# In-place weight sums in the MLP and convolution, and a one-step normalisation after the convolution

## The chip, the core and the metric

The kernel runs on one core of a Trainium2 chip. The metric is the device time of one execution in microseconds. Before the change it is 2091.16 us (median of three runs, 2089.38 to 2091.38). The engines of the core are named as the profile names them: PE is TensorE (matrix products and transposes), DVE is VectorE, ACT is ScalarE, POOL is GpSimd, and SP is SyncE, which here only issues transfers.

## The reference

The model is a two-layer decoder trunk over 1024 tokens of width 1024, in float32. Layer 0 mixes tokens with a causal convolution module, layer 1 with sliding-window attention. Both are followed by a layer norm, a squared-ReLU MLP of width 4096, a second norm and a gated extra embedding. The parts that the change touches:

```python
h = x @ w_in + b_in
a, gate = jnp.split(h, 2, axis=-1)
h = a * jax.nn.sigmoid(gate)
h = depthwise_causal_conv(h, w_dw) + b_dw            # width 31
h = jax.nn.silu(layer_norm(h, ln_g, ln_b))           # the convolution's norm
y = h @ w_out + b_out
...
mlp = jnp.square(jax.nn.relu(x @ w_up)) @ w_down
```

with `layer_norm(x) = (x - mean) * rsqrt(var + 1e-5) * g + b`.

## The kernel before

**Products.** Each float32 operand is split into a rounded high part and a rest (`wh` and `wl` for weights, `xh` and `xl` for activations), and each product is made of three passes: high by high, high by low and low by high. So every weight tile passes through ACT (the cast to `wh`) and DVE (the subtraction `raw - wh`, which gives `wl`) before PE can use it. In the input product of the convolution and in the MLP's up product two blocks of weights are handled as a pair by a Strassen-like scheme with seven products instead of eight. That scheme needs sums of the pair's raw tiles.

**A pair of weights.** `pair_units` (line 1457) gives four units of work, `u0` to `u3`; a unit is one `wh` and one `wl` tile of 128 x 1024. The pair's tiles `raw[0]` and `raw[1]` are of 128 x 1024 too, and L and R are their left and right halves of 512 columns. `u0` splits `raw[0]` as it is, `u1` forms the first two sums, `u2` the third and fourth, `u3` splits the right half of `raw[1]`. Before the change all four sums go to tiles of 128 x 512 of the pool `g`, which has four slots; the pool `raw` has two. The inner function `slot` (line 1463) casts and subtracts each source by itself, so `u1` and `u2` cost two casts and two subtractions of 512 columns each. In the MLP five early pairs of blocks (`EARLY`, 0 to 8) make their `u0` product ahead of the rest; their `u1` loads both raw tiles anew (`again`). A unit's tiles come from rings of five slots.

**The order of products in the MLP.** For a pair, PE multiplies `u1`'s left half with the token form `T[2]` (tiles named X), `u2`'s left half with `T[3]` (E), `u1`'s right half with `T[1]` (A), `u2`'s right half with a plain quarter (`xh`, `xl`) and `u3` with `T[4]` (B): five groups of twelve matmuls, and two more groups for `u0` where the pair isn't early.

**The convolution's norm.** `conv_ln` (line 1264) runs once per pair of token tiles (four pairs, `t0` = 0, 2, 4, 6). A tile consists of two halves of 512 channels, `q` = 0 (tiles named X) and `q` = 1 (tiles named A). `stats` (line 741) takes the mean and variance with two BN_STATS and one BN_AGGR on DVE, adds epsilon and raises to -0.5 on POOL, and then makes the second scalar, -mean * rstd, with one SCALAR_TENSOR_TENSOR of 128 x 1 on DVE. Each half is then scaled in place as `z * rstd + (-mean * rstd)`, `q` = 0 on DVE and `q` = 1 on POOL. PE transposes the scaled halves, ACT applies Silu with the norm's gain and bias, and `xh` and `xl` come from DVE and ACT. Around that place PE fills its time with the product of the extra embedding (`wh`, `wl` by `wh`, `wl`) until the first blocks of the mixer's output product (`wh` by `xh`) can start.

**What sets the order.** Nothing is written out by hand. The program records all operations with their dependences, tile allocations among them, and a list scheduler (`schedule`, with the costs in `cost`) simulates the engines and gives each one a fixed order. Priority is the place in the program, moved by `later`, `after` and `slack`. A tile of a ring is allocated when the simulated schedule frees its slot. So an operation that is removed or shortened, or a tile that is held longer, can move what comes behind it on every engine. All recorded instructions carry one line in the profile, L496; they are told apart by tile names.

Of the kernel before, what the change touches and what calls it, by code (L numbers as in the profile page):

```python
# [13 lines left out]
ALU = mybir.AluOpType  # L14
# [6 lines left out]
HT = 512  # L21
# [507 lines left out]
class Emit:  # L529
# [208 lines left out]
            nc.tensor.matmul(ps, lh, rl, start=False, stop=False, **kw)  # L738
            nc.tensor.matmul(ps, ll, rh, start=False, stop=stop and i == n - 1, **kw)

    def stats(self, halves):

        nc = self.nc
        st = self.small(12).rearrange("p (a b) -> p a b", a=2)
        for i, s in enumerate(halves):
            nc.vector.bn_stats(st[:, i, :], s)
        mv = self.small(2)
        nc.vector.bn_aggr(mv, st)
        rs = self.small(2)
        nc.gpsimd.tensor_scalar(  # L750
            out=rs[:, 0:1], in0=mv[:, 1:2], scalar1=1.0, scalar2=EPS, op0=ALU.mult, op1=ALU.add
        )
        nc.gpsimd.tensor_tensor(out=rs[:, 0:1], in0=rs[:, 0:1], in1=self.mhalf, op=ALU.pow)
        nc.vector.scalar_tensor_tensor(
            out=rs[:, 1:2], in0=mv[:, 0:1], scalar=-1.0, in1=rs[:, 0:1], op0=ALU.mult, op1=ALU.mult
        )
        return rs
# [178 lines left out]
    def conv(self):  # L936

        nc, d, ws = self.nc, self.d, self.ws
# [325 lines left out]
        def conv_ln(t0):  # L1264

            zs = []
            for t in (t0, t0 + 1):
                z = [Z[t // 4, t % 4, q] for q in range(2)]
                rs = self.stats(z)
                for q in range(2):  # L1270
                    (nc.gpsimd if q else nc.vector).tensor_scalar(out=z[q], in0=z[q], scalar1=rs[:, 0:1], scalar2=rs[:, 1:2], op0=ALU.mult, op1=ALU.add)
                zs.append(z)
            for f in range(0, KB, 2):
                blk = [slice((f + j) % 4 * P, ((f + j) % 4 + 1) * P) for j in range(2)]
# [169 lines left out]
    def pair_units(self, aps, again=False):  # L1444

        nc = self.nc
# [3 lines left out]
        def slot(srcs, parts):  # L1450
            wh = nc.tile("wh", (P, 1024), F32R)
            wl = nc.tile("wl", (P, 1024), F32R)
            for s, c in zip(srcs, parts):
                nc.scalar.copy(wh[:, c], s)
                nc.vector.tensor_tensor(out=wl[:, c], in0=s, in1=wh[:, c].bitcast(F32), op=ALU.subtract)
            return wh, wl
# [19 lines left out]
            return slot((S[2], S[1]), (L, R))  # L1476

        def u2():
            S[3], S[4] = self.sb("g"), self.sb("g")
            nc.vector.tensor_tensor(out=S[3], in0=raw[0][:, L], in1=raw[1][:, L], op=ALU.subtract)  # L1480
            nc.vector.tensor_tensor(out=S[4], in0=raw[0][:, R], in1=S[2], op=ALU.subtract)
            return slot((S[3], S[4]), (L, R))

        def u3():
            return slot((raw[1][:, R],), (L,))
# [897 lines left out]
```

## Time and profile before

| what | value |
|---|---|
| three runs | 2091.38, 2091.16, 2089.38 us |
| the profiled execution: time / span | 2088.0 / 2086.3 us |
| busy PE, DVE, ACT, POOL | 2077.3, 1688.4, 1228.1, 279.1 us |
| matmuls and transposes on PE | 9784 |
| convolution up to its norm | 0 to about 256 us |
| the norm and the start of the mixer's output product | about 256 to 285 us |
| up product of the first MLP | about 370 to 690 us |
| up product of the second MLP | about 1395 to 1735 us |

The span runs from the first to the last instruction. The windows view gives, for each stretch, the busy time of each engine with its count of instructions in brackets, then the granted PE clock, the share of the DMA engines and the rate. The timeline view gives start, duration, engine, operation, output and inputs, form and count; what stands in square brackets is the idle time of the engine ahead of the row and what ended it. Matmuls overlap, so a row's duration is longer than the distance from one start to the next.

### The profile page before, as it was taken

How to read it: one execution, taken by the hardware profiler on the slowest of the kernel's cores; microseconds unless marked ns; L12 is line 12 of the kernel's file. 1: busy time of each engine (PE TensorE's matmuls, PEld its weight loads, DVE VectorE, ACT ScalarE, POOL GpSimd, SP SyncE). 2: the span in 40 equal slices, each digit the busy share in tenths (PEclk: the TensorE clock that was granted, in tenths of full speed). 3: DMA queues.
4: the chain of work that ended last, by engine and by line, in shares of the span. 5: the costliest groups of instructions: out<-in, count | busy, mean ns of one | idle time of the engine just before them, and what ended most of it. 6: DMA issues, size and time to landing. Idle time of an engine off the chain costs nothing.

```text
span 2086.3 us, 29471 instructions
## 1 busy us (share of the span) xinstructions
PE 2077.3 (100%) x9784; PEld 1730.8 (83%) x9784; DVE 1688.4 (81%) x2628; ACT 1228.1 (59%) x2268; POOL 279.1 (13%) x512
## 2 busy tenths in 40 slices
PE   9999999999999999999999999999999999999999
PEld 7888888888888888888888888888888888888877
DVE  8999796978876789986983677879888778888688
ACT  6777656856655644454752678866665663333374
POOL 0524121000000000001220356500000000000041
PEclk9999999999999999999999999999999999999999
DMA  6669855988986879876468685598788886575636
GB/s 227 189 205 300 284 192 183 341 289 284 305 308 192 309 269 316 274 261 244 166 219 296 230 291 195 190 337 301 274 295 299 287 298 202 185 245 171 237 112 206
DMA packets 249864, 521.96 MB, mean 250 GB/s; under 512 B 25456, under 2 KB 64112, under 8 KB 249712
## 3 DMA queue, kind: packets, MB, share of 16 engines
q1 hardware_dynamic: 246544, 517.99, 73.3%
q10 hardware_dynamic: 3168, 2.10, 0.3%
q8 instruction: 77, 1.26, 0.2%
q14 instruction: 75, 0.61, 0.1%
HBM read 348.81 MB, written 168.56 MB: 248 GB/s over the span
## 4 chain that ended last, share of the span: by engine, by line
PE 94%; ACT 2%; DVE 2%; DMA 1%; POOL 1%; issue 0%; SPq 0%; DVEq 0%; ACTq 0%
PE ps L496 71%; PE tr L496 23%; ACT z L496 1%; POOL sm L496 1%; ACT t L496 0%; DVE z L496 0%; DMA z<-in_w_dw_dram 0%; DMA A<-in_w_up_dram 0%; DMA mid<-A 0%; DVE B L496 0%; ACT xh L496 0%; DVE E L496 0%; POOL A L496 0%; DMA X<-in_xT_dram 0%; DVE t L496 0%
## 5 line engine op out<-in xcount | busy, mean ns | idle before, releaser
L496 PE MATMUL ps<-xh 128*128 128x512 f32 x618 | 240.4, 389 | 0.0
L496 PE MATMUL ps<-xl,xh 128*128 128x512 f32 x618 | 240.4, 389 | 0.0
L496 PE MATMUL ps<-xh,xl 128*128 128x512 f32 x618 | 240.4, 389 | 0.0
L496 POOL TENSOR_SCALAR sm<-sm 128x1 f32<-128x1 f32 x72 | 26.3, 368 | 1395.2 <-DVE E L496 1208.8
L496 PE MATMUL ps<-xh,wh 128*128 128x512 f32 x520 | 203.3, 393 | 0.8 <-ACT xh L496 0.5
L496 PE MATMUL ps<-xh,wl 128*128 128x512 f32 x520 | 203.4, 392 | 0.0
L496 PE MATMUL ps<-xl,wh 128*128 128x512 f32 x520 | 203.3, 391 | 0.0
L496 ACT CAST wh<-raw 128x1024 fp32r<-128x1024 f32 (+2 forms) x134 | 119.8, 894 | 84.0 <-PE ps L496 46.2
L496 PE MATMUL ps<-wh,xh 128*128 128x512 f32 (+1 forms) x368 | 144.7, 394 | 1.4 <-DVE t L496 0.9
L496 PE MATMUL ps<-wl,xh 128*128 128x512 f32 (+1 forms) x368 | 144.6, 393 | 0.0
L496 PE MATMUL ps<-wh,xl 128*128 128x512 f32 (+1 forms) x368 | 144.4, 392 | 0.0
L496 DVE TENSOR_TENSOR wl<-raw,wh 128x1024 fp32r<-128x1024 f32 (+2 forms) x100 | 98.7, 989 | 52.9 <-ACT wh L496 52.4
L496 ACT CAST wh<-g 128x512 fp32r<-128x512 f32 x136 | 81.1, 619 | 95.2 <-PE ps L496 41.0
L496 PEld LDWEIGHTS ps<-xl,xh 128*128 128x128 f32 x618 | 116.0, 188 | 24.2
L496 PEld LDWEIGHTS ps<-xh,xl 128*128 128x128 f32 x618 | 116.0, 188 | 24.0
L496 PEld LDWEIGHTS ps<-xh 128*128 128x128 f32 x618 | 116.0, 188 | 24.0
L496 ACT CAST xh<-wh 128x1024 fp32r<-128x1024 f32 x76 | 79.8, 1050 | 94.0 <-PE ps L496 56.0
L496 PEld LDWEIGHTS ps<-xh,wh 128*128 128x128 f32 x520 | 97.9, 188 | 21.2 <-ACT xh L496 0.9
L496 PEld LDWEIGHTS ps<-xl,wh 128*128 128x128 f32 x520 | 97.8, 188 | 20.4 <-DVE xl L496 0.8
L496 PEld LDWEIGHTS ps<-xh,wl 128*128 128x128 f32 x520 | 97.7, 188 | 19.8
L496 DVE TENSOR_TENSOR xl<-wh,xh 128x1024 fp32r<-128x1024 f32 x76 | 92.7, 1220 | 25.9 <-ACT xh L496 25.7
L496 ACT ACTIVATE t<-t 128x512 f32<-128x512 f32 x144 | 90.9, 632 | 35.1 <-DVE t L496 33.4
(408 smaller groups left out, 5641.1 us busy)
## 6 DMA issues: line engine op xcount, KB each, us to landing
wh<-hid SPq DMA_DIRECT2D x78, 512.0 KB, 4.7
raw<-in_w_up_dram SPq DMA_DIRECT2D x68, 512.0 KB, 4.4
wl<-in_w_down_dram SPq DMA_DIRECT2D x58, 512.0 KB, 5.3
hid<-zz SPq DMA_DIRECT2D x96, 256.0 KB, 4.8
hid<-t SPq DMA_DIRECT2D x64, 256.0 KB, 4.8
z<-in_w_dw_dram SPq DMA_DIRECT2D x56, 288.0 KB, 4.2
raw<-hid SPq DMA_DIRECT2D x30, 512.0 KB, 4.9
A<-mid SPq DMA_DIRECT2D x48, 256.0 KB, 4.7
```

What stands on the lines that cost most here:

```text
L496: getattr(getattr(nc, o.eng), o.name)(*a, **k)
```

## The change

Three edits:

- `stats` gets an option `centred`, under which it gives the mean and rstd and leaves out the SCALAR_TENSOR_TENSOR.
- `conv_ln` uses it: each half is scaled in one step as `(z - mean) * rstd`. For the first pair of tiles (`t0` = 0) both halves are scaled on DVE; for the others `q` = 1 stays on POOL.
- `u2` writes the third and fourth sums into `raw[0]` itself instead of two `g` tiles, and `slot` then casts and splits `raw[0]` as one tile of 1024 columns.

```diff
-    def stats(self, halves):
+    def stats(self, halves, centred=False):
...
         nc.gpsimd.tensor_tensor(out=rs[:, 0:1], in0=rs[:, 0:1], in1=self.mhalf, op=ALU.pow)
+        if centred:
+            return mv[:, 0:1], rs[:, 0:1]
         nc.vector.scalar_tensor_tensor(
             out=rs[:, 1:2], in0=mv[:, 0:1], scalar=-1.0, in1=rs[:, 0:1], op0=ALU.mult, op1=ALU.mult
         )
...
-                rs = self.stats(z)
+                mean, rstd = self.stats(z, True)
                 for q in range(2):
-                    (nc.gpsimd if q else nc.vector).tensor_scalar(out=z[q], in0=z[q], scalar1=rs[:, 0:1], scalar2=rs[:, 1:2], op0=ALU.mult, op1=ALU.add)
+                    (nc.gpsimd if q and t0 else nc.vector).tensor_scalar(out=z[q], in0=z[q], scalar1=mean, scalar2=rstd, op0=ALU.subtract, op1=ALU.mult)
...
         def u2():
-            S[3], S[4] = self.sb("g"), self.sb("g")
-            nc.vector.tensor_tensor(out=S[3], in0=raw[0][:, L], in1=raw[1][:, L], op=ALU.subtract)
-            nc.vector.tensor_tensor(out=S[4], in0=raw[0][:, R], in1=S[2], op=ALU.subtract)
-            return slot((S[3], S[4]), (L, R))
+            nc.vector.tensor_tensor(out=raw[0][:, L], in0=raw[0][:, L], in1=raw[1][:, L], op=ALU.subtract)
+            nc.vector.tensor_tensor(out=raw[0][:, R], in0=raw[0][:, R], in1=S[2], op=ALU.subtract)
+            return slot((raw[0],), (slice(0, 2 * HT),))
```

The built programs differ in their order over three stretches, by the times that the rows have in the profile before: about 40 to 314 us, 410 to 738 us and 1432 to 1736 us. Outside of them each engine has the same rows in the same order, apart from the numbers of buffers and which of two PSUM pools a bank came from. The places below show the three that the prediction speaks of.

DVE, at the norm of the first pair of tiles, before. `sm` tiles hold the statistics; X and A tiles are the two halves; the first row copies a convolution result out of PSUM.

```order
L496 COPY A_597_2244<-tr_714_2999 128x64
L496 SCALAR_TENSOR_TENSOR sm_63_127<-sm_62_126,sm_63_127 128x1
L496 BN_AGGR sm_68_132<-sm_67_131 128x2
L496 BN_STATS sm_70_134<-A_584_2173 128x6
L496 TENSOR_SCALAR X_592_2202<-X_592_2202,sm_63_127 128x512
L496 SCALAR_TENSOR_TENSOR sm_66_130<-sm_65_129,sm_66_130 128x1
L496 BN_AGGR sm_71_135<-sm_70_134 128x2
L496 BN_STATS sm_73_137<-A_585_2177 128x6
L496 TENSOR_SCALAR X_593_2205<-X_593_2205,sm_66_130 128x512
```

The same place with the change:

```order
L496 COPY A_587_2223<-tr_702_2967 128x64
L496 TENSOR_SCALAR X_583_2181<-X_583_2181,sm_62_126,sm_63_127 128x512
L496 TENSOR_SCALAR A_565_2118<-A_565_2118,sm_62_126,sm_63_127 128x512
L496 TENSOR_SCALAR X_584_2186<-X_584_2186,sm_65_129,sm_66_130 128x512
L496 TENSOR_SCALAR A_566_2122<-A_566_2122,sm_65_129,sm_66_130 128x512
L496 BN_AGGR sm_68_132<-sm_67_131 128x2
L496 BN_STATS sm_70_134<-A_575_2156 128x6
L496 BN_STATS sm_73_137<-A_577_2161 128x6
L496 TENSOR_SCALAR X_595_2248<-X_595_2248,sm_68_132,sm_69_133 128x512
```

The four scalings of the first pair now stand together, ahead of the statistics of the second pair, which stood between them before.

PE, at the end of the fill and the second pair's first transposes, before (`ps_734` is the fill, `ps_765` and `tr_768` are transposes, `ps_739` is the output product):

```order
L496 MATMUL tr_744_3163<-ident_303,A_574_2137 128x128
L496 MATMUL tr_744_3163<-ident_303,A_573_2135 128x128
L496 MATMUL tr_744_3163<-ident_303,A_574_2137 128x128
L496 MATMUL ps_734_3103<-wl_663_2647,wh_661_2644 128x512
L496 MATMUL ps_734_3103<-wh_666_2668,wl_618_2353 128x512
L496 MATMUL ps_765_3249<-ident_303,A_573_2135 128x128
```

and with the change (`ps_724` is the fill, `tr_749` the transposes):

```order
L496 MATMUL tr_733_3147<-ident_303,A_566_2122 128x128
L496 MATMUL ps_724_3086<-wh_658_2652,wh_603_2299 128x512
L496 MATMUL ps_724_3086<-wl_654_2634,wh_603_2299 128x512
L496 MATMUL ps_724_3086<-wh_658_2652,wl_596_2250 128x512
L496 MATMUL ps_724_3086<-wh_658_2652,wh_652_2630 128x512
L496 MATMUL ps_724_3086<-wl_654_2634,wh_652_2630 128x512
L496 MATMUL ps_724_3086<-wh_658_2652,wl_611_2359 128x512
L496 MATMUL tr_749_3213<-ident_303,A_565_2118 128x128
```

Two matmuls of the fill stood between the first group of transposes and the next one; now there are six, since that group comes earlier.

DVE, at the early pair of the first MLP whose first sum stands at 443.24 us in the profile, before:

```order
L496 TENSOR_TENSOR g_1048_4914<-raw_1055_4951 128x512
L496 TENSOR_TENSOR g_1051_4933<-raw_1049_4921,raw_1055_4951 128x512
L496 TENSOR_TENSOR g_1050_4927<-g_1048_4914,raw_1049_4921 128x512
L496 TENSOR_TENSOR wl_1058_4976<-g_1048_4914,wh_1057_4973 128x512
L496 TENSOR_TENSOR g_1054_4942<-raw_1049_4921,g_1050_4927 128x512
L496 TENSOR_TENSOR wl_1058_4976<-g_1050_4927,wh_1057_4973 128x512
L496 TENSOR_TENSOR wl_1061_4997<-g_1051_4933,wh_1060_4995 128x512
L496 TENSOR_TENSOR wl_1061_4997<-g_1054_4942,wh_1060_4995 128x512
```

and with the change:

```order
L496 TENSOR_TENSOR g_1019_4730<-raw_1041_4920 128x512
L496 TENSOR_TENSOR g_1020_4747<-g_1019_4730,raw_1040_4909 128x512
L496 TENSOR_TENSOR raw_1040_4909<-raw_1040_4909,raw_1041_4920 128x512
L496 TENSOR_TENSOR wl_1044_4937<-g_1019_4730,wh_1043_4935 128x512
L496 TENSOR_TENSOR wl_1044_4937<-g_1020_4747,wh_1043_4935 128x512
L496 TENSOR_TENSOR raw_1040_4909<-raw_1040_4909,g_1020_4747 128x512
L496 TENSOR_TENSOR zz_1049_4970<-z_1002_4602,bo_826_3620 128x512
L496 TENSOR_TENSOR wl_1052_5018<-raw_1041_4920,wh_1051_5016 128x512
L496 TENSOR_TENSOR zz_1049_4970<-zz_1049_4970,t_1013_4673 128x512
L496 TENSOR_TENSOR wl_1047_4960<-raw_1040_4909,wh_1046_4958 128x1024
```

`wl` of `u2` (`wl_1061` before, `wl_1047` now) was the eighth row from the first sum at the latest, in two pieces; now it is the tenth, in one piece of 1024 columns.

## The prediction

> **What bounds the kernel now.** First the page's busy times and its chain of waits:
>
> ```profile
> span 2086.3 us, 29471 instructions
> PE 2077.3 (100%) x9784; PEld 1730.8 (83%) x9784; DVE 1688.4 (81%) x2628; ACT 1228.1 (59%) x2268; POOL 279.1 (13%) x512
> PE 94%; ACT 2%; DVE 2%; DMA 1%; POOL 1%; issue 0%; SPq 0%; DVEq 0%; ACTq 0%
> ```
>
> PE is busy for 2077.3 of 2086.3 us, so only 9.0 us are open, and the change takes no matmul away. It can gain only where PE waits. The windows view shows where that is (stretch, length, busy time of PE with its count, of the weight loads, DVE, ACT, POOL):
>
> ```profile
> 250.00:300.00 50.00, 49.12 (x248) 40.07 (x247) 47.28 (x96) 30.22 (x62) 18.70 (x24) 1.00 0.59 202
> 370.00:640.00 270.00, 270.00 (x1195) 223.49 (x1194) 225.30 (x356) 176.47 (x306) 0.00 (x0) 1.00 0.87 298
> 1395.00:1620.00 225.00, 225.00 (x994) 185.99 (x993) 193.47 (x308) 147.62 (x255) 0.00 (x0) 1.00 0.86 293
> 2040.00:2087.00 47.00, 42.15 (x198) 35.18 (x196) 36.01 (x57) 18.55 (x30) 7.79 (x5) 0.97 0.57 193
> ```
>
> In the two up products PE has no idle time: 270.00 us hold 1195 matmuls, one per 0.226 us, and 225.00 us hold 994, again 0.226. Nothing can be gained there. 4.85 us of the 9.0 lie in the last stretch, which the change leaves as it is. The norm's stretch has 0.88 us of idle PE, and the timeline of PE shows what it costs in all:
>
> ```profile
> 259.40 0.40 PE L496 MATMUL ps<-wh,wl 128*128 128x512 f32 x1
> 260.24 0.66 PE L496 MATMUL ps<-ident,A 128*128 128x128 f32 x4 [0.45 <-ACT t L496]
> 260.74 0.62 PE L496 MATMUL tr<-ident,X 128*128 128x128 f32 x4
> 261.70 0.50 PE L496 MATMUL ps<-wh,xh 128*128 128x512 f32 x1 [0.34 <-DVE xh L496]
> 262.50 0.60 PE L496 MATMUL tr<-ident,X 128*128 128x128 f32 x4
> 263.13 0.50 PE L496 MATMUL ps<-wh,xl 128*128 128x512 f32 x1
> 264.42 0.60 PE L496 MATMUL ps<-ident,A 128*128 128x128 f32 x4
> 264.86 0.60 PE L496 MATMUL tr<-ident,A 128*128 128x128 f32 x4
> 265.21 0.47 PE L496 MATMUL ps<-wh,xl 128*128 128x512 f32 x1
> 276.62 0.86 PE L496 MATMUL ps<-wh,xh 128*128 128x512 f32 x3
> 277.53 0.55 PE L496 MATMUL tr<-ident,A 128*128 128x128 f32 x3
> ```
>
> A group of four transposes that nothing holds up takes 0.35 us to the next start (264.86 to 265.21), a matmul 0.23. So 259.40 to 260.24 holds 0.61 us of waiting, 260.74 to 261.70 another 0.61, 262.50 to 263.13 another 0.28: 1.50 us, all for the first pair's norm, once the embedding's fill is used up. At 277.53 come 0.23 more (three matmuls from 276.62 take 0.68), behind the last POOL scaling (its row below: 274.29 + 3.19 = 277.48). Sum: 1.73 us.
>
> **The norm.** What the first pair waits for stands on DVE, POOL and ACT:
>
> ```profile
> 254.12 0.56 POOL L496 TENSOR_TENSOR sm<-sm,sm 128x1 f32<-128x1 f32 x1
> 254.23 0.15 DVE L496 SCALAR_TENSOR_TENSOR sm<-sm,sm 128x1 f32<-128x1 f32 x1
> 254.68 0.77 POOL L496 TENSOR_SCALAR A<-A,sm 128x512 f32<-128x512 f32 x1
> 254.97 0.75 DVE L496 TENSOR_SCALAR X<-X,sm 128x512 f32<-128x512 f32 x1
> 256.38 0.55 DVE L496 TENSOR_SCALAR X<-X,sm 128x512 f32<-128x512 f32 x1
> 256.40 1.01 POOL L496 TENSOR_SCALAR A<-A,sm 128x512 f32<-128x512 f32 x1
> 258.71 0.56 ACT L496 ACTIVATE t<-ps,cst 128x256 f32<-128x256 f32 x1 [0.67 <-PE ps L496]
> 274.29 3.19 POOL L496 TENSOR_SCALAR A<-A,sm 128x512 f32<-128x512 f32 x1 [0.36 <-ACT wh L496]
> ```
>
> Before, the four scalings of the pair end at 255.45 (A), 255.72 (X), 256.93 (X) and 257.41 (A). The new order lets the first start when DVE has done its last copy; the SCALAR_TENSOR_TENSOR stood right behind that copy, at 254.23, so I take 254.3, with four scalings in a row. I cost each at 0.55, the undisturbed row at 256.38; so they end at about 254.85, 255.4, 255.95 and 256.5. The second tile's power ends at 254.68 on POOL, in time for the third. The last is ready 0.9 us earlier, and Silu, which waited for PE (258.71, 0.67 idle), can follow. PE then has six fill matmuls instead of two behind the first transposes: 4 x 0.23 = 0.9 us that cover what was waited for.
>
> The cost: the two new scalings take 1.1 us of DVE ahead of the second pair's statistics, whose aggregate goes from just behind 254.23 to about 256.5. Queued behind it are POOL's power and the second pair's scalings, for which PE waits next, with its transposes of X at 260.74. Against that stand the eight SCALAR_TENSOR_TENSORs that go (0.15 us each, and a handover from POOL to DVE and back). Bounds: all 1.50 us go, or none, as the second pair is late by what the first gains. I take two thirds, 1.0 us, nearest to the 0.9 worked out twice above. At 277.53 the new order puts the late POOL scaling's transposes some 30 instructions later, so its 0.23 us go; the bound is that they stay. Sum: -1.2 us, between 0 and -1.73.
>
> POOL's scaling of 128 x 512 takes 0.77 us at 254.68 and 3.19 at 274.29. The Trainium skill ("SBUF — State Buffer", "Who interferes with whom") explains such a spread by one port pair that DVE and POOL share as an exclusive lock; by that rule the moved scalings also lose their chance of a delay of up to 2.4 us, but in this profile the first pair's had none, so the sum is the same by it. The trace agrees as far as these two rows go.
>
> **The sums in place.** Both forms have their rows (groups by form):
>
> ```profile
> L496 DVE TENSOR_TENSOR wl<-g,wh 128x512 fp32r<-128x512 f32 x136 | 91.4, 696 | 18.8 <-ACT wh L496 18.7
> L496 DVE TENSOR_TENSOR wl<-raw,wh 128x1024 fp32r<-128x1024 f32 x58 | 71.4, 1234 | 22.3 <-ACT wh L496 21.9
> L496 ACT CAST wh<-raw 128x1024 fp32r<-128x1024 f32 x89 | 93.7, 1053 | 63.3 <-PE ps L496 33.4 <-DMA raw<-in_w_gate_dram 11.2 <-PE tr L496 5.4
> L496 ACT CAST wh<-g 128x512 fp32r<-128x512 f32 x136 | 81.1, 619 | 95.2 <-PE ps L496 41.0 <-DVE g L496 28.0 <-PE tr L496 25.9
> L496 DVE TENSOR_TENSOR g<-raw,raw 128x512 f32<-128x512 f32 x34 | 24.0, 705 | 0.0
> ```
>
> There are 34 pairs (third sums, last row). Each exchanges two `wl` of 696 ns for one of 1234, which saves 158 ns of DVE, and two casts of 619 for one of 1053, which saves 185 of ACT: 5.4 and 6.3 us in all. In the up products PE hides both completely, since it has no idle time to give back; so the gain is 0. The sums themselves cost what they did. The transfer that refills `raw[0]` waits for the long `wl` now instead of the fourth sum; it is hidden as long as the second raw tile, whose release doesn't change, comes last anyway.
>
> What can cost something is lateness. At the tightest early pair of the first MLP:
>
> ```profile
> 443.24 0.69 DVE L496 TENSOR_TENSOR g<-raw 128x512 f32<-128x512 f32 x1
> 446.25 1.96 DVE L496 TENSOR_TENSOR wl<-g,wh 128x512 fp32r<-128x512 f32 x3
> 446.60 0.62 PE L496 MATMUL ps<-X,wh 128*128 128x512 f32 x2
> 447.28 0.39 PE L496 MATMUL ps<-X,wl 128*128 128x512 f32 x1
> ```
>
> PE takes `u1`'s `wl` at 447.28, 0.34 us after it ended (446.25 + 0.69). `u2` is complete at 448.21, 4.97 us after the first sum. With the change nine rows at 0.60 stand ahead of its `wl`, which takes 1.23: 6.7 us, 1.7 later. But in the new order its first matmul is the 37th from `u1`'s first one: 36 x 0.226 = 8.1 us, on top of the 3.36 from 443.24 to 446.60, so it is wanted 11.5 us after the first sum. Cover: 4.8 us. I take 0.
>
> **Rivals.**
>
> *The merged unit comes late (slower).* One cast and one subtraction of 1024 can't start before both sums are there, and both halves are ready only at the end. For it: margins like the 0.34 us above. Against it: the cover of 4.8 us. It decides once that cover is gone, that is when `u1` or the raw tiles are themselves that much late. The price is 1.7 us for each early pair whose unit has three sums to make anew, seven in both MLPs: 11.9 us at most. Three of them late: +5.1 us, 2091.2 - 1.2 + 5.1 = 2095.1. The Trainium skill ("Perfetto Trace Analysis", "Optimizing Scalar/DVE Operations") speaks for this: where these engines aren't saturated but cause bubbles, it advises to break instructions up. The trace has DVE busy for 225.30 of 270.00 us there, and no bubble so far.
>
> *The norm gives nothing.* The second pair, behind two more scalings on DVE, is late by about what the first gains. For it: DVE is busy for 47.28 of 50.00 us there. Against it: its first transposes come behind four more fill matmuls. Time: 2091.2, or up to 0.5 more.
>
> *More than the norm goes.* The new order also removes waits in other parts of the three stretches that it rebuilds. The waits of PE view sums them all over the span:
>
> ```profile
> PE ps L496 <- DVE t L496: 2.4, 2, 1.5
> PE ps L496 <- DVE z L496: 0.6, 3, 0.2
> PE ps L496 <- ACT xh L496: 0.5, 1, 0.5
> ```
>
> The largest, 2.4, is the start and one place near the end, outside of these stretches. So at most about 2 us are in reach, 2089.0; a gain of 4 us needs luck in the runs too.
>
> **How the numbers follow.** The profiled execution took 2088.0 us, 1.7 more than its span; with -1.2 it would be 2086.8. The median of the runs shown is 3.2 above it, so I go by the median: 2091.16 - 1.2 = 2090.0. A change within 0.2%, 4.2 us, is about what a measurement of this kernel can't tell from none. The forecast holds 0.62; the norm that gives nothing 0.19, also within 0.2%; the late unit 0.12, slower; the larger gain 0.07, all of which I count as faster. So faster 0.07, same 0.81, slower 0.12. Range: from 2087.0, 3 us under the forecast (1.73 us of waits at most instead of 1.2, and the spread of the three runs, 2.0), to 2094.5, just under three late units.
>
> **What would show it.** Right: one run of four scalings on DVE near 254 to 256.5, PE's gaps between 259 and 264 shrunk from 1.50 to about 0.5, none at 277, and 0.226 us per matmul in both up products. The eight SCALAR_TENSOR_TENSOR rows gone without an earlier Silu would refute the norm's step; PE waiting for `wl` or `wh` between 410 and 470 or 1432 and 1480 would mean the late unit; PE waits for other tiles in the rebuilt stretches, of over 2 us together, a cause that I don't have.

## The result and the profile after

| | median | lowest to highest | runs |
|---|---|---|---|
| before | 2089.98 us | 2087.43 to 2091.38 | 6 |
| changed | 2099.56 us | 2098.99 to 2105.85 | 6 |

Three of the six runs of before are those told above. The change makes the kernel slower by 0.51% (ratio 1.0051, 95% interval 1.0040 to 1.0062), some 10 us. The forecast was 2090.0 us, with a range up to 2094.5. The page of the changed kernel answers to the one shown of before:

```profile
span 2097.5 us, 29424 instructions
PE 2081.1 (99%) x9784; PEld 1730.8 (83%) x9784; DVE 1689.3 (81%) x2588; ACT 1224.9 (58%) x2234; POOL 288.0 (14%) x510
PE 84%; DVE 5%; DMA 4%; ACT 3%; issue 2%; POOL 1%; SPq 0%; ACTq 0%; DVEq 0%; POOLq 0%
```

The span is 11.2 us longer. PE was idle for 9.0 us and is for 16.4. In the chain of waits PE's share falls from 94 to 84%, and those of DVE and DMA grow, from 2 to 5% and from 1 to 4%. ACT has 34 instructions less, as the merging promised, but only 3.2 us less work where the prediction had 6.3. Yet DVE and POOL are busy for longer, DVE with 40 instructions fewer. The windows view (columns as before) and the waits of PE (total, times, longest):

```profile
250.00:300.00 50.00, 47.15 (x246) 38.66 (x245) 44.57 (x85) 33.69 (x70) 22.63 (x22) 1.00 0.65 224
370.00:640.00 270.00, 269.26 (x1190) 221.04 (x1190) 222.49 (x340) 174.86 (x293) 1.45 (x4) 1.00 0.87 300
1395.00:1620.00 225.00, 223.50 (x992) 184.39 (x992) 191.77 (x298) 146.94 (x246) 1.81 (x4) 1.00 0.85 295
```

```profile
PE ps L496 <- ACT t L496: 2.7, 4, 1.2
PE ps L496 <- DVE E L496: 1.5, 2, 0.8
PE ps L496 <- DVE X L496: 1.3, 1, 1.3
PE ps L496 <- POOL A L496: 1.3, 1, 1.3
```

The up products have idle time now. Of the waits shown, three are new, and "ACT t" was one of 0.4 us before. "ACT t" is a PSUM bank (a bank of the memory that PE writes its results to) that ACT copies out too late; 1.7 of the 2.7 us lie in the up products and 1.0 in the convolution. X and A are the two halves of the norm; E here is a table of filter taps in the convolution.

Both traces have 9784 PE instructions. Where one of them starts later than the one of the same number before, time was lost ahead of it. Read so, the 11.2 us fall into four places: 4.6 in the convolution (28 to 256 us by the times of before), 2.0 in the norm's stretch (256 to 289), 2.4 in the first up product (386 to 681), 1.8 in the second (1413 to 1640), and 0.4 elsewhere. I use the same four places for every run; one profiled execution stands behind each, and that of before was a quick one (2088.0 us), so a kernel that is as fast as before can read +1 to +2 in all.

### The profile page after: what moved, and what is told of

Its sections match the earlier page's. It is cut to its first block, busy times and chain, and to the rows that moved or that the text cites. A ratio compares the mean times of both kernels' runs of the same rounds, so it can differ in the third digit from the quotient of the medians.

```text
span 2097.5 us, 29424 instructions
## 1 busy us (share of the span) xinstructions
PE 2081.1 (99%) x9784; PEld 1730.8 (83%) x9784; DVE 1689.3 (81%) x2588; ACT 1224.9 (58%) x2234; POOL 288.0 (14%) x510
## 4 chain that ended last, share of the span: by engine, by line
PE 84%; DVE 5%; DMA 4%; ACT 3%; issue 2%; POOL 1%; SPq 0%; ACTq 0%; DVEq 0%; POOLq 0%
PE ps L496 69%; PE tr L496 15%; DMA raw<-in_w_up_dram 1%; DVE g L496 1%; DMA hid<-zz 1%; DVE wl L496 1%; POOL sm L496 1%; ACT z L496 1%; DVE t L496 1%; ACT wh L496 1%; DMA kept<-t 0%; DVE zz L496 0%; DVE z L496 0%; DVE E L496 0%; DMA t<-proj 0%
## 5 line engine op out<-in xcount | busy, mean ns | idle before, releaser
L496 ACT CAST wh<-raw 128x1024 fp32r<-128x1024 f32 (+2 forms) x168 | 155.1, 925 | 147.7 <-PE ps L496 93.2
L496 PE MATMUL ps<-xh,wh 128*128 128x512 f32 x600 | 235.1, 393 | 1.0 <-ACT t L496 1.0
L496 PE MATMUL ps<-xl,wh 128*128 128x512 f32 x600 | 235.2, 392 | 0.0
L496 PE MATMUL ps<-xh,wl 128*128 128x512 f32 x600 | 235.1, 392 | 0.0
L496 DVE TENSOR_TENSOR wl<-raw,wh 128x1024 fp32r<-128x1024 f32 (+2 forms) x134 | 141.0, 1054 | 68.2 <-ACT wh L496 67.4
L496 PE MATMUL ps<-wh,xh 128*128 128x512 f32 x448 | 176.8, 395 | 0.2 <-DVE xl L496 0.2
L496 PE MATMUL ps<-wl,xh 128*128 128x512 f32 x448 | 176.2, 394 | 0.0
L496 PE MATMUL ps<-wh,xl 128*128 128x512 f32 x448 | 175.8, 393 | 0.1
L496 PEld LDWEIGHTS ps<-xh,wh 128*128 128x128 f32 x600 | 113.2, 189 | 23.8 <-ACT t L496 1.1
L496 DVE TENSOR_TENSOR t<-t,ps 128x512 f32<-128x512 f32 (+1 forms) x105 | 71.9, 684 | 39.5 <-PE ps L496 27.7
```

The costliest lines, as they stand in the source:

```text
L496: getattr(getattr(nc, o.eng), o.name)(*a, **k)
```

## The experiments

Theories at the start. **O**: the new order costs the time, not the instructions. **U**: the sums in place cost it, in any order. **N**: the centred form is slow on POOL and costs the norm's part. To tell O from U, some kernels keep a foreign order: a second recording of another version is scheduled, and each engine follows its order, an instruction being put off only as far as its data or its buffer force it.

| run | what it is | ratio to before (95%) | conv. | norm | up 1 | up 2 |
|---|---|---|---|---|---|---|
| the change | | 1.0051 (1.0040 to 1.0062) | 4.6 | 2.0 | 2.4 | 1.8 |
| sums_own | sums in place and merged only | 1.0045 (1.0033 to 1.0058) | 6.5 | 0.2 | 2.8 | 1.6 |
| norm_own | norm's edit only | 1.0023 (1.0014 to 1.0031) | 3.3 | 1.8 | 0.0 | 0.8 |
| a_in_b | all edits, order of before | 1.0116 (1.0103 to 1.0130) | 6.3 | 3.0 | 7.4 | 8.3 |
| b_in_a | no edit, order of the change | 1.0057 (1.0043 to 1.0070) | 11.3 | 0.9 | 1.6 | 0.7 |
| norm_in_b | norm's edit, order of before | 1.0016 (1.0007 to 1.0025) | 0.7 | 3.2 | 0.1 | -0.3 |
| dve_in_b | first pair on DVE, old form, order of before | 0.9999 (0.9990 to 1.0008) | 0.8 | 0.0 | 0.3 | 0.5 |
| halves_in_b | sums in raw[0], not merged, order of before | 1.0081 (1.0068 to 1.0093) | 2.8 | -0.1 | 8.4 | 5.9 |
| third_ctl | sums_own with another use of g tiles | 1.0081 (1.0068 to 1.0095) | 11.9 | 1.2 | 4.6 | 1.5 |
| third | the same and a third raw tile | 1.0060 (1.0047 to 1.0074) | 11.0 | 2.6 | 0.0 | -0.3 |
| shake_dve | no edit, DVE's cost 1 ns up | 1.0000 (0.9991 to 1.0009) | 2.1 | 0.5 | 0.1 | 0.0 |
| shake_act | no edit, ACT's cost 1 ns up | 1.0002 (0.9993 to 1.0011) | 1.1 | -0.1 | 0.1 | 0.6 |
| raw1_in_b | third sum in raw[1], order of before | 1.0005 (0.9996 to 1.0014) | 1.2 | -0.1 | 0.1 | 0.3 |
| halves_own | sums in raw[0], not merged | 1.0023 (1.0014 to 1.0033) | 3.3 | -1.6 | 3.7 | 0.0 |
| mlp_only | in place and merged in the MLPs only | 1.0021 (1.0012 to 1.0030) | 1.3 | -0.1 | 2.1 | 2.0 |
| dve_own | first pair on DVE, old form | 1.0006 (0.9997 to 1.0015) | 0.9 | 0.9 | 0.2 | 0.2 |
| tap_dve | sums_own, one POOL addition on DVE | 1.0032 (1.0019 to 1.0044) | 4.6 | 0.1 | 2.1 | 1.2 |

The last four columns are us lost at the four places. "Own" means that the scheduler made its own order. In five of these executions the granted clock fell to 0.50 for 3.4 us at a time (the end of the span left aside), and half of 3.4 us, 1.7, can be lost by that alone: once in the convolution of sums_own, a_in_b and third, twice in that of b_in_a and third_ctl, once more in the norm's stretch of third and in the second up product of a_in_b.

**Order or instructions: four runs.** The first two carry one edit each, with the hunks of the diff above; the other two cross edits and orders:

```diff
         self.program()
+        if ORDER_OF is not None:
+            other = Emit(tc, self.d, ORDER_OF)
+            other.program()
+            self.nc.force = [(o.key, o.eng) for o in other.nc.schedule() if o.eng != "alloc"]
```

> Only the third and fourth sums in place and their merged split; the norm as before. The scheduler makes its own order. Three theories stand: O, the order that the scheduler makes costs the time; U, the merged units cost it, in whatever order; N, the norm's POOL scalings cost their part of it. O and U both expect +7 to +10 us (about 4.5 up to 256 us, 2.4 in the first up product, 1.8 in the second, little in the norm). If this is under +4, the loss belongs to the norm's edit, which no theory of mine says.

> Only the norm's edit; the sums as before, scheduler's own order. N: +1 to +3 us, all between 250 and 295 us, with POOL's 128 x 512 scalings at 2.2 us or more each against 1.4 on average before. Rival: the norm gains what I predicted (-1.2) and the 2 us seen in its stretch come from the order of the rest; then -2 to 0. In the conv stage before 250 us and in both up products nothing changes, by both.

> All edits of the change, but each engine is made to keep the order that it had before: an instruction is moved only as far back as its data or its buffer force it (a merged split stands where the second half's split stood, the loads that refill raw tiles go a few places back, the moved A scalings stand right behind the X scaling of the same tile). O: within 0.2% of before, +0 to +2.5 us, where what is over 0 lies in the norm's stretch (N); nothing in the conv stage and the up products. U: +7 to +11 us, in the same stretches as with the change.

> The reverse: no edit at all, the instructions of before (four g sums, two casts and two subtractions, the norm's mult and add with POOL's A scalings), but each engine is made to follow the order of the changed kernel; the two extra splits stand right ahead of the second ones. O: slower by +7 to +11 us, in the conv stage (4.5) and the up products (4) as with the change, and without the 2 us in the norm's stretch if N holds. U: within 0.2%, -1 to +2 us.

The sums alone cost nearly as much as the whole change (+9.4 us at 2090 us), the norm alone +4.8. Then O and U both failed in their simple form: the edits in the order of before lose 24 us, not 0 to 2.5 (O) or 7 to 11 (U), and the old instructions in the new order lose 11 to 12, where U had -1 to +2. Each order suits its own instructions; next to the 24 us, the scheduler's new order had won back more than half. So I asked for a pure change of order:

```diff
-        t = 120.0 if isinstance(o.kw.get("scalar"), View) else 70.0
+        t = 120.0 if isinstance(o.kw.get("scalar"), View) else 71.0
```

and, in the other kernel, `60.0 + f * 0.85` for ACT as `61.0 + f * 0.85`.

> The kernel before with no instruction changed; only the scheduler's cost of a DVE instruction is 1 ns higher (71 instead of 70 ns and the columns). Its order differs from before over about as many rows as that of the change. O (a new order costs time by itself, since the old one was picked among many): +2 to +10 us, mainly up to 300 us. Rival (the order costs only where the changed instructions don't fit it): -2 to +2 us.

> The same with the scheduler's cost of an ACT instruction 1 ns higher (61 instead of 60). O: +2 to +10 us, mainly up to 300 us, not at the same places as with the other. Rival: -2 to +2 us.

Both kernels have new orders (compared by operation and tile, 632 and 471 of the 2628 rows of DVE before don't fit into one order with theirs, with the change 854), and neither costs anything. So a new order needn't cost, and O has fallen as the account of the whole: what costs is something in the instructions, which no order that was tried hides wholly. It hasn't fallen as a part. norm_own loses 3.3 us in the convolution, where its instructions are those of before and where none of my theories expected a loss; the two shaken kernels read 2.1 and 1.1 there, and norm_in_b 0.7. That stays open.

**The norm's form on POOL.**

```diff
+        for n, (s1, s2, o0, o1) in forms.items():
+            nc.gpsimd.tensor_scalar(out=t[n], in0=t[n], scalar1=s1, scalar2=s2, op0=o0, op1=o1)
```

> Leaves the whole computation out; the output is zero. POOL scales tiles of 128 x 512 in five forms in turn (mult and add with two scalars of one tile, the same with scalars of two tiles, subtract and mult likewise, and mult and add with constants), four times over: first with DVE idle, then while DVE runs 100 scalings (mult and add), 100 centred scalings, 90 subtractions of two tiles, 90 BN_STATS, 150 copies. N: subtract and mult takes over 2 us with DVE idle too, mult and add about 0.77. Rival (the port that DVE and POOL share): all forms alike with DVE idle, about 0.8, and all slowed alike to 2 us or more beside the subtractions, not beside one-source work.

Rows of POOL from its timeline, and groups by form (`submul` is subtract and mult, `madd` mult and add; `c` once: both scalars from one tile, twice: from two tiles):

```profile
3.70 0.77 POOL L496 TENSOR_SCALAR madd<-madd,c 128x512 f32<-128x512 f32 x1 [1.95 <-DMA madd<-in_x_dram]
6.20 2.08 POOL L496 TENSOR_SCALAR submul<-submul,c 128x512 f32<-128x512 f32 x1 [0.99 <-DMA submul<-in_x_dram]
...
L496 POOL TENSOR_SCALAR submul<-submul,c,c 128x512 f32<-128x512 f32 x24 | 53.9, 2248 | 0.0
L496 POOL TENSOR_SCALAR madd<-madd,c,c 128x512 f32<-128x512 f32 x24 | 22.3, 930 | 0.0
```

POOL needs 2.08 us for subtract and mult with DVE idle (DVE started at 9.75) and 0.77 for mult and add; 2.25 and 0.93 on average over 24 each, nearly all of them beside DVE's scalings. Whether the scalars lie in one tile or in two makes no difference. On DVE the two forms cost the same, 746 and 743 ns. POOL ran through its list faster than planned, so only its last rows fell beside DVE's subtractions; those were 0.3 us longer (2.50 and 2.57 us for subtract and mult). So the form is slower on POOL by itself. In the kernel:

```diff
-                    (nc.gpsimd if q else nc.vector).tensor_scalar(out=z[q], in0=z[q], scalar1=rs[:, 0:1], scalar2=rs[:, 1:2], op0=ALU.mult, op1=ALU.add)
+                    (nc.gpsimd if q and t0 else nc.vector).tensor_scalar(out=z[q], in0=z[q], scalar1=rs[:, 0:1], scalar2=rs[:, 1:2], op0=ALU.mult, op1=ALU.add)
```

This is the edit of dve_in_b and, in its own order, of dve_own; norm_in_b has the norm's hunks of the change.

> The norm's edit alone (centred, first pair on DVE), with each engine in the order of before; the moved scalings stand behind the X scaling of the same tile. N (the centred form is slow on POOL, 2.6 us on average instead of 1.4): +1 to +3 us, all between 255 and 292 us, and nothing in the conv stage, where the norm's edit in its own order lost 3.1 us with the same instructions as before. Rival: the form doesn't matter and the order did it all; then -1.5 to +0.5 us.

> Only the move of the first pair's two A scalings to DVE, in the old form (mult and add, with the SCALAR_TENSOR_TENSORs), in the order of before. N: POOL's other six scalings stay at about 1.4 us on average, and the time is -1.5 to +0.5 us. Rival (DVE has no room for the two scalings, or the scalings on POOL are slowed by DVE): +1 us or more, with POOL's scalings at over 2 us here too.

> No edit but the first pair's A scalings on DVE, in the old form of mult and add with their SCALAR_TENSOR_TENSORs; sums as before; the scheduler's own order. With POOL's scalings at their old duration my sum for the norm can be tried by itself: -1.2 us (0 to -1.7) if it was right but for POOL's form; -0.5 to +1 us if the second pair is late by what the first gains, as one rival had it.

The groups of POOL's scalings by form, of before, the change, norm_in_b and dve_in_b in this order:

```profile
L496 POOL TENSOR_SCALAR A<-A,sm 128x512 f32<-128x512 f32 x8 | 11.2, 1397 | 1.6 <-ACT t L496 0.8 <-DVE sm L496 0.4 <-ACT wh L496 0.4
```

```profile
L496 POOL TENSOR_SCALAR A<-A,sm,sm 128x512 f32<-128x512 f32 x6 | 15.8, 2632 | 0.4
```

```profile
L543 POOL TENSOR_SCALAR A<-A,sm,sm 128x512 f32<-128x512 f32 x6 | 17.9, 2983 | 0.5 <-POOL sm L543 0.2
```

```profile
L543 POOL TENSOR_SCALAR A<-A,sm 128x512 f32<-128x512 f32 x6 | 9.4, 1562 | 2.9 <-DVE sm L543 1.7 <-ACT t L543 0.8 <-ACT wh L543 0.4
```

In the order of before the norm's edit loses 3.2 us in its stretch, and the same move in the old form loses nothing there. That shows N. But the move gains nothing either, and in its own order it reads +0.9, with PE waiting for POOL instead:

```profile
PE tr L543 <- POOL A L543: 1.4, 1, 1.4
```

In the changed kernel the price shows at the second pair (timeline of POOL, DVE and PE):

```profile
258.92 0.54 DVE L496 TENSOR_SCALAR X<-X,sm,sm 128x512 f32<-128x512 f32 x1
...
260.28 0.54 DVE L496 TENSOR_SCALAR A<-A,sm,sm 128x512 f32<-128x512 f32 x1
...
261.97 2.37 POOL L496 TENSOR_SCALAR A<-A,sm,sm 128x512 f32<-128x512 f32 x1
264.96 1.18 POOL L496 TENSOR_TENSOR sm<-sm,sm 128x1 f32<-128x1 f32 x2
265.56 0.55 DVE L496 TENSOR_SCALAR X<-X,sm,sm 128x512 f32<-128x512 f32 x1 [1.69 <-POOL sm L496]
```

The four scalings stand in a row as foreseen. Then POOL is held in one scaling for 2.37 us, the next tile's power on POOL stands behind it, and DVE waits 1.69 us for that power; PE's 1.3 us for X follow from it.

**The hold of raw[0].** Before, raw[0] is free once the fourth sum has been read from it; with the change it is held until the merged split. Two kernels in the order of before separate the hold from the merging: both sums in raw[0] but cast and split as halves (halves_in_b), and the third sum in raw[1], which `u3` holds anyway (raw1_in_b):

```diff
-            S[3], S[4] = self.sb("g"), self.sb("g")
+            S[3], S[4] = raw[0][:, L], raw[0][:, R]
...
-            S[3], S[4] = self.sb("g"), self.sb("g")
+            S[3] = raw[1][:, L]
+            S[4] = self.sb("g")
```

> The third and fourth sums in place, but cast and split as two halves of 512 as before, in the order of before; the norm as before. With the whole change in this order the loss was 24 us, about 21 of it in the conv stage and the up products. Theory H: it is the hold; raw[0] is free only after the second split and no more after the fourth sum, its refill starts later, and DVE waits for it with ACT and the PSUM copies queued behind. Then +12 to +21 us here too. Theory M: it is the merged unit, whose one cast and one split of 1024 can't start before both sums. Then 0 to +4 us here.

> In the order of before: the third sum is written in place into the left half of raw[1], which nothing reads behind it and which is held until u3's split anyway; the fourth goes to a g tile as before; two casts and two splits; the norm as before. H (only the longer hold of a raw tile costs): -1.5 to +1.5 us, against +16 for both sums in raw[0]. Rival (writing in place costs by itself, since the sum must wait for the readers of its own tile): +5 us or more.

halves_in_b loses 16 us by its medians, 14.3 of it in the up products, where the whole change in that order loses 15.7. raw1_in_b loses nothing that can be told. So what costs in the up products is neither the writing in place nor the merging, whose 1.4 us at most are no more than the one fall of the clock there in a_in_b (halves_in_b has none): it is the hold. The same pair on DVE and on SP's queue, before:

```profile
1494.00 0.69 DVE L496 TENSOR_TENSOR g<-raw,g 128x512 f32<-128x512 f32 x1
...
1494.71 0.33 SPq L496 DMA_DIRECT2D raw<-in_w_up_dram  x1
```

and with all edits in the same order (a_in_b), on ACT and PE too:

```profile
1510.45 0.69 DVE L543 TENSOR_TENSOR g<-raw 128x512 f32<-128x512 f32 x1 [1.85 <-DMA raw<-in_w_up_dram]
...
1515.63 0.68 DVE L543 TENSOR_TENSOR raw<-raw,g 128x512 f32<-128x512 f32 x1
...
1520.30 1.23 DVE L543 TENSOR_TENSOR wl<-raw,wh 128x1024 fp32r<-128x1024 f32 x1 [1.57 <-ACT wh L543]
...
1521.55 0.33 SPq L543 DMA_DIRECT2D raw<-in_w_up_dram  x1
...
1511.24 0.62 ACT L543 CAST wh<-g 128x512 fp32r<-128x512 f32 x1 [1.31 <-DVE g L543]
...
1514.60 0.59 ACT L543 COPY t<-ps 128x512 f32<-128x512 f32 x1 [1.36 <-DVE v L543]
...
1515.24 0.73 PE L543 MATMUL ps<-A,wh 128*128 128x512 f32 x2 [1.77 <-ACT t L543]
```

Before, the refill of raw[0] is issued 0.02 us after the fourth sum's end (1494.69), and 8.8 us ahead of that of raw[1] (1503.51). In a_in_b the sum ends at 1516.31, the merged split at 1521.53, and the refill goes out at 1521.55: 5.2 us later, and only 4.3 us ahead of the next one (1525.83).

The 1.85 us on DVE are those of this pair's own first sum, which reads raw[1]. Its load was late by way of SP's queue. `u3`'s split of the pair before had freed the tile at 1503.98, but the load went out at 1505.71: the held refill of raw[0] (issued at 1500.29) stood ahead of a store (mid<-A, 1500.67), and the load of raw[1] behind the reading back of that store (A<-mid), for which SP waited until 1505.30. So the first sum came late, ACT's casts waited for it in turn, ACT's copy of a PSUM bank stood behind them, and PE waited 1.77 us for the bank. PE never waits for raw itself: in the up products of a_in_b 7.6 us of its waits are for "ACT t" and 1.4 for `wh`.

In the changed kernel's own order the held tile is at some pairs the last to come free. So it is at the early pair that the prediction took as the tightest (DVE and SP's queue):

```profile
454.54 0.68 DVE L496 TENSOR_TENSOR wl<-raw,wh 128x512 fp32r<-128x512 f32 x1
...
455.75 1.22 DVE L496 TENSOR_TENSOR wl<-raw,wh 128x1024 fp32r<-128x1024 f32 x1
...
456.99 0.33 SPq L496 DMA_DIRECT2D raw<-in_w_up_dram  x1
...
462.51 0.69 DVE L496 TENSOR_TENSOR g<-raw 128x512 f32<-128x512 f32 x1 [2.35 <-DMA raw<-in_w_up_dram]
```

`u3`'s split of raw[1] ends at 455.22, the merged split of raw[0] at 456.97, and the load that goes out 0.02 us later is the one that the next pair's first sum waits for. Of the 12.4 us that DVE and ACT wait for raw loads in the two up products of this kernel, in twelve waits, 4.7 us (three waits) are for loads that a merged split released; the others follow `u3`'s split, and how the hold reaches each of them was not followed.

The counter-proof is a third raw tile. It takes 4 KB of each partition; to have them, two g tiles become one tile of 1024 (gg), which serves as raw tile in the up products. The control has gg without that service.

```diff
+        nc.move("gg", "raw")
         banks = {}
...
+        nc.move("raw", "gg")
         self.x = []
```

> Control for the next kernel. The sums in place and merged as in the change, the norm as before, the scheduler's own order; but two of the four g tiles of 512 are one tile of 1024 (gg) now, which holds the two sums of the filter taps in the convolution, half of the third token forms of the down product, half of the norm's gain and bias and every second pair of query parts. raw keeps two tiles. Theory H (the hold of raw[0] delays its refill): the two up products lose 3 to 6 us together, as in the run with the sums alone (4.5), with DVE and ACT waiting for raw loads for 8 to 15 us in 370 to 690 us. The conv stage may come out anywhere between 0 and +8 us, since its order changes again.

> The same, but during each up product the tile gg serves as a third raw tile, so a refill needn't wait for the merged split. H: DVE and ACT wait for raw loads for under 3 us in 370 to 690 us, and the up products lose 0 to 1 us together; 2.5 to 5 us faster than the control. Theory M (the merged unit itself comes late): the up products lose as much as in the control.

The third tile takes the loss of the up products from 6.1 to -0.3 us, and the kernel from 2107.36 to 2102.06 us. What DVE and ACT wait for raw loads in 370 to 690 us, in before, the change (two rows), the control (two rows) and with the third tile (two rows):

```profile
DVE g L496 <- DMA raw<-in_w_up_dram: 0.2, 1, 0.2
```

```profile
DVE g L496 <- DMA raw<-in_w_up_dram: 6.7, 6, 2.3
ACT wh L496 <- DMA raw<-in_w_up_dram: 1.9, 1, 1.9
```

```profile
DVE g L543 <- DMA raw<-in_w_up_dram: 7.4, 6, 2.6
ACT wh L543 <- DMA raw<-in_w_up_dram: 5.0, 2, 3.4
```

```profile
DVE g L543 <- DMA raw<-in_w_up_dram: 2.1, 2, 1.4
DVE g L543 <- DMA gg<-in_w_up_dram: 1.9, 1, 1.9
```

0.2 us before, 8.6 with the change, 12.4 in the control, 4.0 with the third tile; I had expected under 3, but these 4.0 no longer reach PE. As the sums stay merged and in place in both, the loss in the up products is shown to be one of the hold. The other use of the g tiles makes the convolution 11 us slower in both, more than the 8 that I had allowed for, so neither is a kernel to keep.

**The convolution.** Its pairs use the same `u2`. Is its loss made there, and by what?

```diff
-            ws.add(... self.pair_units([d["w_in2"][c - ALONE, k] for k in range(2)]))
+            ws.add(... self.pair_units([d["w_in2"][c - ALONE, k] for k in range(2)], sums=False))
```

This is mlp_only, with `sums=False` keeping the old `u2`; halves_own is the first hunk of the diff for the hold, in the scheduler's own order.

> Sums in place and merged in the two MLPs only; the pairs of the convolution and the norm as before; the scheduler's own order. If the loss is made where the pairs are: within 1.5 us of before up to 370 us, +3 to +6 us in the up products, in all +3 to +6.5. If the convolution's loss were an order that the rest of the program forces on it: +3 us or more up to 256 us here too.

> Both sums in raw[0], cast and split as halves of 512, norm as before, in the scheduler's own order. If the convolution's loss is one of merging: under +2 us up to 256 us (sums alone, merged: 6.2), and in the up products +3 to +6 us as with the merged units, from the hold. If it is the hold there too: +4 to +7 us up to 256 us.

With the convolution's pairs left alone its loss is 1.3 us, within what a new order reads; with merged pairs it is 6.5. So most of it comes from these pairs. Halves read 3.3, between the two answers that I had named, and norm_own read as much with the old pairs; so how it divides between the hold and the merging isn't shown. By the medians, halves in place lose 4.7 us in all and merged units 9.8. In the changed kernel and in sums_own the largest piece, 2.6 and 4.1 us between 141 and 159 us, hangs on one instruction of POOL. Before and in the changed kernel:

```profile
139.94 1.12 POOL L496 TENSOR_TENSOR g<-cst,z 128x256 f32<-128x256 f32 x1 [8.35 <-DVE wl L496]
```

```profile
142.26 3.66 POOL L496 TENSOR_TENSOR g<-cst,z 128x256 f32<-128x256 f32 x1 [1.53 <-DVE wl L496]
...
145.25 2.62 DVE L496 SCALAR_TENSOR_TENSOR g<-B,cst,g 128x512 f32<-128x512 f32 x3
...
145.95 0.60 ACT L496 ACTIVATE cst<-B,cst 128x256 f32<-128x256 f32 x1 [3.15 <-POOL g L496]
...
151.15 0.69 DVE L496 TENSOR_TENSOR g<-g,ps 64x512 f32<-64x512 f32 x1 [3.29 <-ACT g L496]
...
153.58 0.66 PE L496 MATMUL tr<-ident,g 128*128 128x128 f32 x4 [0.73 <-DVE g L496]
...
155.31 0.50 PE L496 MATMUL ps<-xh,wh 128*128 128x512 f32 x1 [0.95 <-ACT t L496]
```

The addition that ends the first half of the filter taps takes 3.66 us instead of 1.12. ACT waits 3.15 us for it, DVE 3.29 us for what is queued behind on ACT, and PE for both. While it ran, DVE worked off instructions on two tiles (TENSOR_TENSOR) without a break, two of them the sums in place, until it turned to SCALAR_TENSOR_TENSOR at 145.25; the addition ended 0.67 us later. In before, sums_own, halves_own and b_in_a too it ended 0.67 to 0.68 us after that turn. My last theory, P, was that POOL can't get at its inputs while DVE subtracts tile from tile.

```diff
-                    nc.gpsimd.tensor_tensor(out=to, in0=acc, in1=out, op=ALU.add)
+                    on = nc.vector if i == TAPS - 1 and f == 0 else nc.gpsimd
+                    on.tensor_tensor(out=to, in0=acc, in1=out, op=ALU.add)
```

```diff
+        for k in range(150):
+            nc.gpsimd.tensor_tensor(out=t["pc"][:, 0:256], in0=t["pa"][:, 0:256], in1=t["pb"][:, 0:256], op=ALU.add)
+        for r in range(2):
+            for k in range(6):
+                nc.vector.tensor_tensor(out=t["sub"], in0=t["x0"], in1=t["x1"], op=ALU.subtract)
...
```

> The run with the sums alone, in the very order that it had; only the one POOL addition that ends the first half of the filter taps (g<-cst,z, 128 x 256, at 142 us) is made on DVE, right ahead of the two sums in place. Theory P (POOL can't get at its inputs while DVE subtracts tile from tile): ACT goes on 2.5 us earlier at 143 us, DVE's wait of 3.3 us at 151 us for ACT shrinks to under 1, PE's waits between 151 and 156 us too, with the slow matmuls behind them; 2 to 4 us less up to 256 us than with the sums alone (+6.3), in all 2095 to 2097.5 us. Rival (ACT's wait is not what PE waits for): 2098.5 to 2100.

> Leaves the whole computation out; the output is zero. POOL adds two tiles of 128 x 256 150 times in a row, while DVE runs, twice over, 6 subtractions of two tiles of 128 x 512, 12 SCALAR_TENSOR_TENSORs with two tiles, 20 scalings, 12 subtractions and 20 copies. P: additions that fall into subtractions take as long as the rest of the run of subtractions (3 to 7 us), all others 0.7 to 1.1. Rival: all additions take 0.7 to 1.5 us, and the 3.66 us in the kernel have another cause.

With that one addition on DVE and everything else in the order of sums_own, the time is 2096.75 us, inside what P gave and outside of what its rival gave, though the intervals of the two ratios still overlap (1.0019 to 1.0044, sums_own 1.0033 to 1.0058). Between 141 and 159 us 1.6 us are lost instead of 4.1, but some 1.6 of these were the slower clock (last section). In the whole convolution it is 4.6 instead of 6.5, just under the 2 to 4 less that P gave. DVE's wait is halved, and not under 1 us:

```profile
144.69 0.60 ACT L544 ACTIVATE cst<-B,cst 128x256 f32<-128x256 f32 x1 [0.35 <-DVE g L544]
...
151.69 0.69 DVE L544 TENSOR_TENSOR g<-g,ps 64x512 f32<-64x512 f32 x1 [1.59 <-ACT g L544]
```

So the late addition costs at this place: some 1 us next to the changed kernel (1.6 against 2.6, both at the full clock), 2.5 next to sums_own. Why it is late is not shown. The measurement by itself (POOL's addition by tile and by form, DVE's subtraction) went against P:

```profile
L496 POOL TENSOR_TENSOR pc<-pa,pb x150: 721/786/1080, 6.3 to 150.3; 128x256 f32<-128x256 f32 x150
```

```profile
L496 DVE TENSOR_TENSOR sub<-x,x 128x512 f32<-128x512 f32 x36 | 39.4, 1093 | 13.6 <-DMA x<-in_x_dram 12.5
```

No addition took more than 1.08 us, whatever DVE did: 1.05 beside its subtractions and beside its SCALAR_TENSOR_TENSORs alike, and 0.72 to 0.79 beside scalings and copies. DVE's subtractions became longer too, 1.09 us where one took 0.71 on average in the other measurement. The Trainium skill ("SBUF — State Buffer", "Who interferes with whom") says that DVE work with two inputs from SBUF contends with POOL's reads, and that the order of issue decides who blocks. The first agrees with these durations. The second might tell the kernel from the measurement, as POOL was first here, with a stream of its own, and came into DVE's stream in the kernel; no run here shows it. Nor does it say why the addition ends once DVE turns to SCALAR_TENSOR_TENSOR, which slowed the additions here as much as subtractions did.

## Why the prediction was wrong, point by point

- **PE sets the end and has no room.** Right. For that very reason each lateness that gets through to PE is paid in full.
- **"So the gain is 0" for the merged units.** Right as far as it goes: ACT got 3.2 us less work, half of the 6.3 that were counted, DVE none (0.9 us more in all), and no gain is seen in the time.
- **"The transfer that refills raw[0] waits for the long wl now instead of the fourth sum; it is hidden as long as the second raw tile, whose release doesn't change, comes last anyway."** This is the step that failed in the up products. Its condition sounded safe, but no row was put under it, and the listing of DVE with the change already showed the opposite: there `u3`'s split of the second raw tile stands two rows ahead of the merged split. So at that pair the held tile comes last, its refill goes out at 456.99, and DVE stands 2.35 us for it. Where the second tile does come last, as in a_in_b, the held refill (5.2 us later) pushes the loads behind it in SP's queue. In both cases the first sum of a pair comes late in DVE's fixed order, with all that is queued behind it. Put at 0, it measured 4.2 us in the changed kernel and 15.7 in the order of before; with a third raw tile it is gone.
- **"Cover: 4.8 us. I take 0."** The cover itself nearly held: in the changed kernel no wait of PE for `wl` or `wh` is among those that its view lists. But I looked for the lateness at PE's own inputs alone. It came as PSUM banks that ACT copied out late. The rival "the merged unit comes late" had named raw tiles that come late, and late they came, by the very hold that the step above called hidden; but by up to 2.35 us, not by the 4.8 that it asked for, and not by its path, PE waiting for `wl` or `wh`. Its 2095.1 us was the nearest of the forecasts, at a chance of 0.12, and near by luck.
- **The norm, -1.2.** The four scalings came as drawn (0.54 us each, in a row). Two things failed. I priced the new form on DVE and left the six scalings that stay on POOL at their old duration; they went from 1.40 to 2.63 us on average. The sum has no such term; with it the norm's stretch loses 2.0 us in the changed kernel, and 3.2 in the order of before. And the 1.0 us for the first pair didn't come even in the old form (0.0 and +0.9 in two orders): the rival that the second pair is late by what the first gains was right there. Where 0.23 us of waiting for a POOL scaling were to go, PE now waits 1.3 us for one.
- **The convolution's pairs.** 34 pairs were counted, but only an early pair of the MLP was looked at. The pairs of the convolution, where POOL, ACT and DVE hand the filter taps to each other, lost most, 4.6 us. The rule that I cited from the Trainium skill ("Perfetto Trace Analysis", "Optimizing Scalar/DVE Operations"), to break instructions up where engines that aren't saturated cause bubbles, agrees with the runs there as far as they go (6.5 merged, 3.3 as halves, one execution each), and hardly in the up products (4.4 and 3.7).
- **"PE waits for other tiles in the rebuilt stretches, of over 2 us together, a cause that I don't have."** This sign of being wrong is the one that appeared. I had weighed the new order only for what it may gain. A new order by itself cost nothing in the two shaken kernels; an order that must work round a longer hold does.

## What to carry to other kernels

An operand that is overwritten in place is held until its last new reader is done: follow the buffer to its refill, and the refill to whoever stands behind it in its queue and first in line for it, before calling the saving free. A form of an instruction has to be priced on every engine that runs it. Where PE has no idle time, a late PSUM copy is as expensive as a late operand, so look along the queue of the engine that empties the banks.

## What the runs showed of the hardware

On POOL, TENSOR_SCALAR with subtract and mult took 2.08 us for 128 x 512 f32 with DVE idle, 2.7 times as long as mult and add (0.77).

A stall of PE can cost about as much again behind it. After the 1.77 us wait in a_in_b the granted clock (the number ahead of the last two) fell to half for 3.4 us (all of the second row and, by its 0.88, 0.4 us of the first). In the 3 us of the second row 9 matmuls started, where 4 us hold some 19 at the full clock:

```profile
1515.20:1517.00 1.80, 1.76 (x7) 1.45 (x8) 1.80 (x4) 0.00 (x0) 0.00 (x0) 0.88 1.05 404
1517.00:1520.00 3.00, 3.00 (x9) 2.32 (x8) 1.73 (x3) 0.78 (x1) 0.00 (x0) 0.50 0.86 320
1520.00:1524.00 4.00, 4.00 (x19) 3.29 (x18) 2.43 (x3) 2.49 (x5) 0.00 (x0) 1.00 0.35 41
...
1555.70:1558.00 2.30, 2.30 (x10) 1.91 (x11) 2.30 (x5) 0.52 (x1) 0.00 (x0) 1.00 1.05 403
```

The last row follows a wait as long (1.74 us, at 1555.68), and its clock stays at 1.00. It is the same with the convolution's stall: behind the same three waits the clock was 0.57 in sums_own (155.20 to 159.20 us) and 1.00 in the changed kernel, and 10 matmuls started there in sums_own, 19 in the changed kernel. That is about the 1.6 us by which sums_own loses more at this place (4.1 against 2.6). The Trainium skill ("TensorE: Matmul & The Clock Gate", "What's actually happening") tells of a window of about 3.4 us that runs freely and halves the clock after an idle one. That the same wait has both outcomes agrees with a free-running window; that it takes a whole window of idleness doesn't, since 1.77 us of waiting were enough in the first place.
